# Low weight parts of layer 1 prepared during layer 0, three more root sums as split pairs, and a planner with trials

## The chip, the cores and the metric

The kernel runs on one core of one Trainium2 chip. The metric is the device time of one execution in microseconds (us). The kernel before was run three times; a profile of one further execution shows what every engine did. Engines are named as the profile names them: PE (TensorE matmul), PEld (its weight loads), DVE (VectorE), ACT (ScalarE), POOL (GpSimd) and SP (SyncE, which issues nearly all DMAs).

## The reference

A decoder trunk of two layers on 1024 tokens of width 1024, all in float32. Cut to what matters:

```python
for l in range(DEPTH):                       # 2 layers
    h = rmsnorm(x, attn_norm[l])
    proj = h @ w_in[l]                       # one input projection, split among four mixers
    y_a = mla_attention(c_q, c_kv, k_r, ...) # a: latent attention with rotary keys
    y_b = short_gated_conv(g_b, g_c, u_conv, conv_w[l])   # b
    y_c = multiscale_pool(u_pool, ...)                    # c
    y_d = swa_sink_attention(q_sw, k_sw, v_sw, ...)       # d: window of 128, with sinks
    groups = stack([y_a, y_b, y_c, y_d])     # each group of 256 channels gets its own RMS norm
    mixed = rms(groups) * mix_norm[l]
    x = x + mixed @ w_o[l]
    h2 = rmsnorm(x, ffn_norm[l])
    gate, up = split(h2 @ w_gate_up[l])
    x = x + (silu(gate) * up) @ w_down[l]
return rmsnorm(x, final_norm)
```

Every RMS norm needs, for each token, the sum of squares over the channels.

## The kernel before

**Layout and precision.** Channels lie on the 128 partitions, tokens along the free axis in two halves of 512. PE multiplies float32 matrices as split pairs: a value f becomes `hi`, its cast to the format fp32r (on ACT), and `lo = f - hi`, also in fp32r (on DVE). `mm3` (L316 to L329) makes a product of three matmuls, hi·hi, hi·lo and lo·hi. Nearly all matmuls of the kernel are issued at L322.

**Weights.** `weights` (L204 to L218) loads a block from DRAM into a place of type F, casts it to `hi` (L216, ACT) and subtracts (L217, DVE) to get `lo`. The blocks of a layer come as a stream in a fixed order (`expect_layer`, L238 to L246): 15 blocks of `w_in` (128 x 1024, 512 KB each; in layer 0 three of them are handled apart at the start), a small one for the rotary key, and 8 blocks of `w_o` (128 x 768, 384 KB). `take` and `ahead` keep one block fetched ahead; `ring_next` keeps the last two split blocks. An input block feeds both token halves, 2 x 8 x 3 = 48 matmuls.

**Places.** 47 places of 128 x 1024 float32 in SBUF hold nearly everything (class `Slots`). Each request takes a place; whoever gets a place waits for its former user.

**Root sums.** `SumSq` (L360 to L418) collects the squares in one tile per token half. `rnorm` then sums over the partitions with a matmul by a matrix of ones and computes the inverse root on ACT and DVE. Without `pair` that matmul is in fp32 (L405); with `pair`, the collected tile is split by a cast and a subtraction, and the sum is two fp32r matmuls (L402). Before the change, pairs are used for group b, the key/value latent, group a, the FFN norm and the norms after the down projection; groups c and d (`group_scale`, L738) and the query latent (`sq_q`, L868) use fp32 in both layers, and so does the first norm of the program.

**Stages of a layer.** The mixers: projections, window attention, convolution and pooling, latent attention, with the output projection in parts between them (`out_part`). Then gate-up, and then the down projection: 28 units (7 terms, B11, B21, N1, N2, T3, T4, B22, of a two-by-two block scheme that saves an eighth of the products, times 4 pairs of output blocks), each of 11 x 3 = 33 matmuls. At unit n the loop (L1784 on) issues the loads of the raw down weights of unit n + 2 (`dn_raw`, L1562), splits those of unit n + 1, fetches the next term's activations (`dn_acts`, L1597), and adds the product to the residual (L1771). In layer 0 the finished residual goes to DRAM (`done`, L1754), and the first three projections of layer 1 start within the last term.

**Order of the work.** Within the program text the order is only a draft. `scheduled_kernel` traces the program, and the class `Order` simulates it with a cost for each instruction (`costs`), a delay for DMA loads, and a model of the DMA's throughput. It lists each engine's instructions by latest start (`run`, `find`), assigns PSUM banks and places from the simulated ends, traces again, four rounds in all, and keeps the round with the shortest simulated span. The order found is imposed on every engine, SP's queue among them. All of this is done before the kernel is compiled.

Of the kernel before, what the change touches and what calls it, by code (L numbers as in the profile page):

```python
# [13 lines left out]
F32 = mybir.dt.float32  # L14
# [5 lines left out]
P = 128  # L20
# [3 lines left out]
HT = 512  # L24
# [11 lines left out]
HALVES = (1, 0)  # L36
OUT_PARTS = tuple((d, t) for d in range(NK) for t in HALVES)
N_U = 47

NSP = 3  # L40
NG = NFF // 2
# [81 lines left out]
def trunk_kernel(ctx: ExitStack, tc: tile.TileContext, ins, out, given=None, ends=None):  # L123
    nc = tc.nc
# [10 lines left out]
    R, F = View(slots, F32R), View(slots, F32)  # L135
# [65 lines left out]
        for i in ring.popleft():  # L201
            R.free_pair(i)

    def weights(src, n):  # L204
        if n > 2 * P:
            s = F.pair()
            raw = F.ap2(s)
            sp.dma_start(raw[:, :n], src)
            hi, lo = (R.ap2(i) for i in ring_next())
            F.free_pair(s)  # L210
        else:
            raw = wpool.tile([P, 2 * P], F32, name="vraw", tag="vraw")
            sp.dma_start(raw[:, :n], src)
            hi = wpool.tile([P, 2 * P], F32R, name="vhi", tag="vhi")
            lo = wpool.tile([P, 2 * P], F32R, name="vlo", tag="vlo")
        act.copy(hi[:, :n], raw[:, :n])  # L216
        dve.tensor_tensor(out=lo[:, :n], in0=raw[:, :n], in1=rd(hi[:, :n]), op=ALU.subtract)  # L217
        return hi, lo  # L218
# [16 lines left out]
    def expect(f, *args):  # L235
        stream.append((f, args))

    def expect_layer(l):  # L238
        for m in (2, 3, 0, 4, 5, 6, 1, 13, 14, 10, 11, 12, None, 7, 8, 9):
            if m is None:  # L240
                expect(rope_weights, l)
            else:
                if l or m not in (2, 3, 0):
                    expect(weights, ins["w_in"][l, m], 2 * HT)
        for d in range(NK):
            expect(weights, ins["w_o"][l, d, :, 2 * P :], 6 * P)  # L246

    def ahead():
        if stream and not fetched:
# [230 lines left out]
    for l in range(L):  # L480
# [256 lines left out]

        def group_scale(g):  # L738

            sg = SumSq(2 * P, g in "b")  # L740
            for t in range(2):
                for c in range(2):
                    sg.add(t, F.ap(y[g][c][t]))
                r = sg.rnorm(t)
                for c in range(2):
                    a = F.ap(y[g][c][t])
                    mul_to(a, a, F.ap(r))
                F.free(r)
# [116 lines left out]
                rope.append(F.half())  # L865
                sp.dma_start(F.ap(rope[-1]), ins[name][:, t * HT : (t + 1) * HT])
        cq = [[None, None], [None, None]]
        sq_q = SumSq(2 * P)  # L868
        for m in range(2):
            pp = project() if m else nextp  # L870
            for t in range(2):
# [909 lines left out]
        fresh = {B11: (0, 0), N1: (1, 1), N2: (0, 1), T4: (1, 0)}  # L1781
        banks = {}
        tail = []
        for n, (c, m) in enumerate(units):  # L1784
            if n + 2 < len(units):
                raws.append(dn_raw(*units[n + 2]))
            if c in fresh:
                u, t = fresh[c]
                d = 2 * m + u
                if not last or t == 0:  # L1790
                    x[d][t] = F.half()
                elif c == N1:
# [24 lines left out]
            evac(c, m, p)  # L1817
            for _ in range(2):
                if cn is not None and m < NM - 1:
                    nxt.extend(dn_acts(cn, (len(nxt) + 1) // 2))  # L1820
            if m == NM - 1:
                cur, nxt = nxt, []
            if c == T3:
                done(2 * m, 0)
            elif c == T4:
                done(2 * m + 1, 0)
                done(2 * m + 1, 1)
            elif c == B22:
                done(2 * m, 1)
                if m == 0:  # L1830
                    expect_layer(l + 1)
                    ahead()
                if m == 1:
                    ratt[0] = ss.rnorm(0, tag="pv")
                if m == NM - 1:
                    ratt[1] = ss.rnorm(1, tag="pv")
# [17 lines left out]
class Order:  # L1854
# [7 lines left out]
    SHARED = 1.3  # L1862
    LEAST = 0.14

    def __init__(self, traced, edges, banks=True):
        self.n = len(traced)
        self.engine = [self.queue(i) for i in traced]
        self.cost = [self.costs(i) for i in traced]
        self.kind = [self.kinds(i) for i in traced]
        self.moved = [self.passing(i) for i in traced]  # L1870
        place = {i.name: k for k, i in enumerate(traced)}
        need = [{} for _ in traced]
        users = self.users = defaultdict(list)
        for k, i in enumerate(traced):
            for m in {a.memref for a in (*i.outs, *i.ins) if hasattr(a, "memref")}:
                users[m].append(k)
        freed = [set() for _ in traced]
        for k, i in enumerate(traced):
            for name, kind in edges(i.name):
                if name in place:  # L1880
                    p = place[name]
                    need[k][p] = need[k].get(p, False) or "NoSync" not in str(kind)
                elif banks or self.engine[k] != "PE":
                    freed[k].update(place[x] for x, _ in edges(name) if x in place)
            for p in freed[k]:
                need[k][p] = True
        for m, ks in users.items():
            made = [freed[k] for k in ks if any(m == getattr(a, "memref", 0) for a in traced[k].outs)]
            for p in set().union(*made).difference(ks):
                for k in ks:  # L1890
                    if p < ks[0]:
                        need[k][p] = True
        self.need = [list(d.items()) for d in need]
        self.feeds = [[] for _ in traced]
        for k, d in enumerate(self.need):
            for p, sync in d:
                self.feeds[p].append((k, sync))
# [79 lines left out]
            return 0.29 + n * 0.00098, 0.21 + n * 0.00098  # L1977
        return t, t - 0.083

    def run(self, rank, back=False):  # L1980

        ahead, wait = (self.need, self.feeds) if back else (self.feeds, self.need)
        late, cost, kind = self.LATE[back], self.cost, self.kind
        left = [len(w) for w in wait]
        ready, end, free = [0.0] * self.n, [0.0] * self.n, dict.fromkeys(self.ENGINES, 0.0)
        later = {e: [] for e in self.ENGINES}
# [14 lines left out]
        for _ in range(self.n):  # L2004
            best = None
            for e in self.ENGINES:
                due(e, free[e])
                if not now[e] and not later[e]:
                    continue
                t = free[e] if now[e] else later[e][0][0]  # L2010
                if e == "SP" and not back and len(flying) == self.LANES:
                    t = max(t, flying[0])
                if best is None or t < best[0]:
                    best = t, e
            t, e = best
            due(e, t)
            k = heapq.heappop(now[e])[1]
            seen, taken = cost[k]
            order[e].append(k)
            if back:  # L2020
                free[e] = t + taken * (self.SHARED if kind[k] == "pool" else 1.0)
# [15 lines left out]
            for j, sync in ahead[k]:  # L2037
# [6 lines left out]
                    r = end[k] + self.HOP[e] if sync else t  # L2044
                ready[j] = max(ready[j], r)
                left[j] -= 1
                if not left[j]:
                    heapq.heappush(later[self.engine[j]], (ready[j], j))
        return end, order

    def find(self, passes=3):
        rank, best = list(range(self.n)), None
        for _ in range(passes):
# [2 lines left out]
                best = max(end), order, end  # L2056
            rank, _ = self.run([-x for x in end], back=True)
        return best

    def tiles(self, prefix):  # L2060

# [33 lines left out]
                )  # L2095


def scheduled_kernel(fresh, ins_of, rounds=4):

# [14 lines left out]
        return nc, traced, asked  # L2114

    nc, traced, asked = trace(None, None)
    plan = Order(traced, nc.dependency_edges)
    end, best = plan.find()[2], None
    for _ in range(rounds):
        given = plan.banks(end), plan.ends(end, asked)  # L2120
        nc, traced, asked = trace(*given)
        plan = Order(traced, nc.dependency_edges)
        span, order, end = plan.find()
        if best is None or span < best[0]:
            best = span, given, order
    return trace(*best[1], best[2])[0]


# [131 lines left out]
```

## Time and profile before

| | us |
|---|---|
| median of 3 runs | 2050.09 |
| lowest and highest | 2048.81, 2051.84 |
| profiled execution, its own time | 2051.07 |
| its span, first to last instruction | 2049.3 |

The profile has a page of totals and several views of the trace. A line of the view by stretches gives the stretch, its length, the busy time of each engine with its count of instructions, the granted PE clock, the DMA share (mean busy share of 16 DMA engines) and the GB/s moved. A line of the waits says who waited for whom, the sum in us, how often, and the longest. A group line has the line of the kernel, engine, operation, names of output and inputs, shapes and count, then the busy time in us and the mean duration in ns, then idle time before it and what ended that. Matmuls are pipelined: one of 512 columns is recorded with some 390 ns while the next one starts earlier, so starts are compared rather than durations.

### The profile page before, as it was taken

How to read it: one execution, taken by the hardware profiler on the slowest of the kernel's cores; microseconds unless marked ns; L12 is line 12 of the kernel's file. 1: busy time of each engine (PE TensorE's matmuls, PEld its weight loads, DVE VectorE, ACT ScalarE, POOL GpSimd, SP SyncE). 2: the span in 40 equal slices, each digit the busy share in tenths (PEclk: the TensorE clock that was granted, in tenths of full speed). 3: DMA queues.
4: the chain of work that ended last, by engine and by line, in shares of the span. 5: the costliest groups of instructions: out<-in, count | busy, mean ns of one | idle time of the engine just before them, and what ended most of it. 6: DMA issues, size and time to landing. Idle time of an engine off the chain costs nothing.

```text
span 2049.3 us, 26536 instructions
## 1 busy us (share of the span) xinstructions
PE 2029.5 (99%) x9422; PEld 1675.6 (82%) x9422; DVE 1521.4 (74%) x2443; ACT 988.8 (48%) x1737; POOL 568.7 (28%) x428
## 2 busy tenths in 40 slices
PE   9999999999999999999999999999999999999998
PEld 7887888878888888888888878888788888888887
DVE  8779978997666768655657898889966666685555
ACT  7447657753333335434433666667433333354342
POOL 0100000047786772000001000000577777710000
PEclk9999999999999999999999999999999999999999
DMA  5431232334555556766424213232455555487552
GB/s 203 97 76 41 74 104 79 141 134 154 199 174 187 180 167 250 269 217 197 157 59 94 52 52 102 74 108 110 150 176 187 176 175 176 162 298 258 178 188 87
DMA packets 144294, 305.51 MB, mean 149 GB/s; under 512 B 13985, under 2 KB 61089, under 8 KB 144161
## 3 DMA queue, kind: packets, MB, share of 16 engines
q1 hardware_dynamic: 139680, 292.27, 41.8%
q0 software_dynamic: 4480, 11.54, 3.2%
q8 instruction: 74, 1.21, 0.2%
q14 instruction: 60, 0.48, 0.1%
HBM read 219.34 MB, written 94.90 MB: 153 GB/s over the span
## 4 chain that ended last, share of the span: by engine, by line
PE 91%; DVE 5%; issue 1%; DMA 1%; ACT 1%; POOL 0%; SPq 0%; DVEq 0%; ACTq 0%; POOLq 0%
PE ps_mm L322 35%; PE ps_s L322 28%; PE ps_t L322 10%; PE ps_pv L322 8%; PE ps_pv L1090 2%; PE ps_t L1078 1%; DVE u L345 1%; PE ps_s L1024 1%; PE ps_s L1026 1%; PE ps_s L1025 1%; DMA u<-in_w_gu 1%; PE ps_s L896 1%; DVE u L348 1%; PE ps_pv L699 1%; PE ps_s L638 1%
## 5 line engine op out<-in xcount | busy, mean ns | idle before, releaser
L322 PE MATMUL ps_mm<-u,u 128*128 128x512 f32 (+1 forms) x3378 | 833.3, 390 | 4.4 <-ACT u L342 1.5
L322 PEld LDWEIGHTS ps_mm<-u,u 128*128 128x128 f32 x3378 | 615.0, 188 | 131.3 <-issue 5.5
L322 PE MATMUL ps_s<-u,u 128*128 128x512 f32 x2670 | 634.4, 390 | 2.8 <-DVE u L345 1.7
L345 DVE TENSOR_TENSOR u<-u,u 128x1024 fp32r<-128x1024 f32 (+2 forms) x400 | 453.3, 1152 | 231.6 <-ACT u L342 161.1
L322 PEld LDWEIGHTS ps_s<-u,u 128*128 128x128 f32 x2670 | 500.4, 188 | 110.8 <-DVE u L345 4.0
L342 ACT CAST u<-u 128x1024 fp32r<-128x1024 f32 (+2 forms) x400 | 345.8, 882 | 456.2 <-PE ps_mm L322 72.1
L322 PE MATMUL ps_t<-u,u 128*128 128x512 f32 (+1 forms) x1124 | 254.2, 378 | 1.1 <-DVE u L1309 1.1
L322 PEld LDWEIGHTS ps_t<-u,u 128*128 128x128 f32 x1124 | 202.1, 188 | 41.7 <-DVE u L1309 1.6
L1502 POOL TENSOR_TENSOR tp<-tp,u 128x512 f32<-128x512 f32 x80 | 126.3, 1579 | 345.0 <-ACT tp L1500 345.0
L322 PE MATMUL ps_pv<-u,u 128*128 128x512 f32 x744 | 177.1, 389 | 0.0
L322 PEld LDWEIGHTS ps_pv<-u,u 128*128 128x128 f32 x744 | 139.6, 188 | 29.1
L296 POOL DMA_DIRECT2D gd<-in_w_gu x24 | 22.1, 921 | 421.5 <-PE ps_t L322 283.9
L1087 POOL MEMSET u<- 128x128 f32 x32 | 6.1, 221 | 431.3 <-PE ps_pv L1090 148.8
L1500 ACT ACTIVATE tp<-tp 128x512 f32<-128x512 f32 x80 | 50.6, 632 | 147.9 <-DVE tp L421 147.8
L347 ACT ACTIVATE u<-u,par 128x512 fp32r<-128x512 f32 x100 | 70.4, 717 | 37.4 <-DVE u L421 11.0
L342 ACT CAST u<-ps_t 128x512 fp32r<-128x512 f32 (+3 forms) x132 | 65.1, 503 | 47.9 <-PE ps_t L1078 26.7
L348 DVE SCALAR_TENSOR_TENSOR u<-u,par,u 128x512 fp32r<-128x512 f32 x100 | 73.3, 745 | 17.6 <-ACT u L347 17.4
L345 DVE TENSOR_TENSOR u<-ps_t,u 128x512 fp32r<-128x512 f32 (+3 forms) x132 | 75.4, 580 | 12.7 <-ACT u L342 10.9
L1580 POOL TENSOR_TENSOR u<-u,u 128x352 f32<-128x352 f32 x64 | 82.7, 1293 | 2.9 <-DMA u<-in_w_dn 1.5
L1580 POOL TENSOR_TENSOR u<-u 128x352 f32<-128x352 f32 x64 | 82.1, 1284 | 4.6 <-DMA u<-in_w_dn 3.9
L386 ACT ACTIVATE tn<-u 128x512 f32<-128x512 f32 (+1 forms) x91 | 52.9, 596 | 57.2 <-DVE u L1771 47.9
L1290 POOL TENSOR_TENSOR u<-u 128x512 f32<-128x512 f32 x38 | 69.5, 1829 | 21.8 <-DVE u L345 21.8
(203 smaller groups left out, 2347.4 us busy)
## 6 DMA issues: line engine op xcount, KB each, us to landing
u<-in_w_gu SPq DMA_DIRECT2D x84, 512.0 KB, 4.2
ad<-u SPq DMA_DIRECT2D x154, 256.0 KB, 2.4
u<-ad SPq DMA_DIRECT2D x70, 512.0 KB, 4.7
u<-in_w_dn SPq DMA_DIRECT2D x64, 352.0 KB, 3.6
qd<-u SPq DMA_DIRECT2D x64, 352.0 KB, 2.6
u<-qd SPq DMA_DIRECT2D x32, 512.0 KB, 5.0
u<-in_w_in SPq DMA_DIRECT2D x28, 512.0 KB, 3.5
u<-in_w_dn SPq DMA_DIRECT2D x24, 512.0 KB, 5.2
```

Of the source, the lines that this page charges most:

```text
L296: paced(pool.dma_start(d, a, **more))
L322: last_mm = pe.matmul(o, w, r, start=start and k == 0 and i == 0, stop=stop and k == n - 1 and i == 2, skip_group_check=again,)
L342: a = act.copy(hi, f)
L345: dve.tensor_tensor(out=lo, in0=f, in1=rd(hi), op=ALU.subtract)
L347: a = act.activation(hi, f, AF.Copy, scale=gain)
L348: dve.scalar_tensor_tensor(out=lo, in0=f, scalar=gain, in1=rd(hi), op0=ALU.mult, op1=ALU.subtract)
L386: act.activation(q, f, AF.Square)
L1090: pe.matmul(py[:, c0:], v_of(j, h), R.ap(s)[:, c0:], start=j == 0 and n == 0, stop=j == nj - 1 and n == 1,)
L1290: pool.tensor_tensor(out=q4, in0=q4, in1=F.ap(self.raw[1] + 1), op=ALU.add)
L1500: last_silu = act.activation(g, g, AF.Silu)
L1502: pool.tensor_tensor(out=g, in0=g, in1=r, op=ALU.mult)
L1580: pool.tensor_tensor(out=o, in0=a, in1=b, op=ALU.add)
```

## The change

It has three parts.

1. `prepare` loads a weight block of layer 1, splits it, and stores its `lo` to a DRAM tile of its own; the `hi` is dropped. The down stage of layer 0 calls it 23 times, for 15 blocks of `w_in` and 8 of `w_o`, about once per unit from unit 2 to unit 26. In layer 1, `weights` then loads the raw block and the stored `lo` by two DMAs, casts `hi` and leaves out the subtraction. Layer 0's own weights are split as before.
2. In layer 1, the root sums of groups c and d and of the query latent are made as split pairs. Each has two token halves.
3. The planner makes one round for each of two assumed speeds (DVE and ACT as modelled, and 3% slower). Each order is then changed at random 30 times, by shifting the ranks of instructions that end shortly before a wait of PE (`improve`), a change being kept if the simulated span is no longer. Of the two, the one with the shorter mean span in six simulations of the fixed order is taken, in which a quarter of the DMA loads are late by up to 2.5 us and the engines' costs vary by 2% (`trial`).

```diff
+SLOW = (1.0, 1.03)
+PREP = (1, 27)
...
+    prepared = {}
+
+    def prepare(key, src, n):
+
+        s, h, lo = F.pair(), R.pair(), R.pair()
+        raw = F.ap2(s)[:, :n]
+        sp.dma_start(raw, src)
+        split(R.ap2(h)[:, :n], R.ap2(lo)[:, :n], raw)
+        F.free_pair(s)
+        R.free_pair(h)
+        prepared[key] = dpool.tile([P, n], F32, name="ph%s%d_%d" % key)
+        sp.dma_start(prepared[key], rd(R.ap2(lo)[:, :n]))
+        R.free_pair(lo)
+
-    def weights(src, n):
+    def weights(src, n, key=None):
         if n > 2 * P:
             s = F.pair()
             raw = F.ap2(s)
             sp.dma_start(raw[:, :n], src)
             hi, lo = (R.ap2(i) for i in ring_next())
             F.free_pair(s)
+            if key in prepared:
+                sp.dma_start(rd(lo[:, :n]), prepared[key])
+                act.copy(hi[:, :n], raw[:, :n])
+                return hi, lo
...
-            sg = SumSq(2 * P, g in "b")
+            sg = SumSq(2 * P, g in ("b", "bcd")[l])
...
-        sq_q = SumSq(2 * P)
+        sq_q = SumSq(2 * P, l > 0)
...
+        todo = deque() if last else deque([*(("in", m) for m in (2, 3, 0, 4, 5, 6, 1, 13, 14, 10, 11, 12, 7, 8, 9)), *(("o", d) for d in range(8))])
         for n, (c, m) in enumerate(units):
+            while not last and n > PREP[0] and len(todo) * (PREP[1] - PREP[0]) > 23 * (PREP[1] - n) and todo:
+                w, i = todo.popleft()
+                src = ins["w_in"][l + 1, i] if w == "in" else ins["w_o"][l + 1, i, :, 2 * P :]
+                prepare((w, l + 1, i), src, 2 * HT if w == "in" else 6 * P)
...
+    def trial(self, order):
+        ends = (self.run(None, fixed=order, draw=random.Random(n))[0] for n in range(6))
+        return sum(map(max, ends)) / 6
...
+    def improve(self, best, tries):
+        draw = random.Random(1)
+        span, order, end = best
+        rank, _ = self.run([-x for x in end], back=True)
+        e, o = self.run(rank)
+        if max(e) <= span:
+            span, order, end = max(e), o, e
+        found = self.waits(order, end)
+        for _ in range(tries):
+            at = draw.choices([t for t, _ in found], [w for _, w in found])[0]
+            new = [
+                r + draw.gauss(0.0, 1) if at - 40 < t < at + 5 else r for r, t in zip(rank, end)
+            ]
+            e, o = self.run(new)
+            if max(e) <= span:
+                rank, span, order, end = new, max(e), o, e
+                found = self.waits(order, end)
+        return span, order, end
...
-def scheduled_kernel(fresh, ins_of, rounds=4):
+def scheduled_kernel(fresh, ins_of, rounds=1):
...
+    for slow in SLOW:
+        plan, asked, first.slow = first, tried, slow
+        end = plan.find()[2]
+        for _ in range(rounds):
+            given = plan.banks(end), plan.ends(end, asked)
+            nc, traced, asked = trace(*given)
+            plan = Order(traced, nc.dependency_edges, slow)
+            best = plan.find()
+            end = best[2]
+            order = plan.improve(best, 30)[1]
+            found.append((plan.trial(order), given, order))
+    best = min(found, key=lambda x: x[0])
     return trace(*best[1], best[2])[0]
```

More of the change, by code (lines that the diff above doesn't have):

```diff
@@ L2 @@
 import math
+import random
 from collections import defaultdict, deque
@@ L243, in expect_layer @@
                 if l or m not in (2, 3, 0):
-                    expect(weights, ins["w_in"][l, m], 2 * HT)
+                    expect(weights, ins["w_in"][l, m], 2 * HT, ("in", l, m))
         for d in range(NK):
-            expect(weights, ins["w_o"][l, d, :, 2 * P :], 6 * P)
+            expect(weights, ins["w_o"][l, d, :, 2 * P :], 6 * P, ("o", l, d))
     def ahead():
@@ L1863, with __init__ @@
     LEAST = 0.14
-    def __init__(self, traced, edges, banks=True):
+    def __init__(self, traced, edges, slow=1.0, banks=True):
+        self.slow = slow
         self.n = len(traced)
@@ L1978, in costs, with run @@
         return t, t - 0.083
-    def run(self, rank, back=False):
+    def run(self, rank, back=False, fixed=None, draw=None):
         ahead, wait = (self.need, self.feeds) if back else (self.feeds, self.need)
         late, cost, kind = self.LATE[back], self.cost, self.kind
+        if fixed is None:
+            cost = [
+                (a * self.slow, b * self.slow) if e in ("DVE", "Activation") else (a, b)
+                for (a, b), e in zip(cost, self.engine)
+            ]
         left = [len(w) for w in wait]
@@ L2006, in run @@
             for e in self.ENGINES:
[L2007 to L2010, printed above, removed]
+                if fixed is not None:
+                    i = len(order[e])
+                    if i == len(fixed[e]) or left[fixed[e][i]]:
+                        continue
+                    t = max(free[e], ready[fixed[e][i]])
+                else:
+                    due(e, free[e])
+                    if not now[e] and not later[e]:
+                        continue
+                    t = free[e] if now[e] else later[e][0][0]
                 if e == "SP" and not back and len(flying) == self.LANES:
@@ L2015, in run @@
             t, e = best
-            due(e, t)
-            k = heapq.heappop(now[e])[1]
-            seen, taken = cost[k]
+            if fixed is not None:
+                k = fixed[e][len(order[e])]
+            else:
+                due(e, t)
+                k = heapq.heappop(now[e])[1]
+            seen, taken = cost[k]
+            if draw:
+                late = 2.5 * draw.random() if draw.random() < 0.25 else 0.0
+                if e in ("DVE", "Activation", "Pool"):
+                    more = draw.gauss(0.0, 0.02) * seen
+                    seen, taken = seen + more, taken + more
             order[e].append(k)
@@ L2046, in run @@
                 left[j] -= 1
-                if not left[j]:
+                if not left[j] and fixed is None:
                     heapq.heappush(later[self.engine[j]], (ready[j], j))
         return end, order
+    def trial(self, order):
+        ends = (self.run(None, fixed=order, draw=random.Random(n))[0] for n in range(6))
+        return sum(map(max, ends)) / 6
     def find(self, passes=3):
@@ L2058, in find, with waits @@
         return best
+    def waits(self, order, end):
+        found, free = [], 0.0
+        for k in order["PE"]:
+            seen, taken = self.cost[k]
+            start = end[k] - seen
+            if start - free > 0.05:
+                found.append((start, start - free))
+            free = start + taken
+        return found
+    def improve(self, best, tries):
[10 more added lines that the diff above has]
+                r + draw.gauss(0.0, 1) if at - 40 < t < at + 5 else r for r, t in zip(rank, end)
+            ]
+            e, o = self.run(new)
[3 more added lines that the diff above has]
+        return span, order, end
     def tiles(self, prefix):
@@ L2116, in scheduled_kernel @@
     nc, traced, asked = trace(None, None)
[L2117 to L2125, printed above, removed]
+    first, tried, found = Order(traced, nc.dependency_edges), asked, []
+    for slow in SLOW:
[10 more added lines that the diff above has]
+    best = min(found, key=lambda x: x[0])
     return trace(*best[1], best[2])[0]
```

## Prediction

> **What bounds the kernel now.** I read the totals of the page first, then its engines by stretch, then the list of TensorE's waits, and only then single instructions.
>
> ```profile
> PE 2029.5 (99%) x9422; PEld 1675.6 (82%) x9422; DVE 1521.4 (74%) x2443; ACT 988.8 (48%) x1737; POOL 568.7 (28%) x428
> PEclk9999999999999999999999999999999999999999
> ```
>
> TensorE (PE) is busy for 2029.5 of 2049.3 us at the full granted clock. Busy time alone does not prove that it runs at its best rate, so the stretches come next: layer 0's mixers (50 to 430), its gate-up stage (450 to 800), its down stage (811 to 1021), the inner part of that, and layer 1's mixers (1021 to 1440). The columns after the length are PE, PEld, DVE, ACT, POOL, then clock, DMA share and GB/s.
>
> ```profile
> 50.00:430.00 380.00, 377.98 (x1851) 311.10 (x1849) 331.27 (x735) 235.60 (x510) 19.78 (x30) 1.00 0.30 87
> 450.00:800.00 350.00, 350.00 (x1541) 288.58 (x1540) 247.59 (x247) 122.49 (x168) 248.74 (x173) 1.00 0.53 180
> 811.00:1021.00 210.00, 210.00 (x928) 173.85 (x927) 128.27 (x154) 96.35 (x127) 1.81 (x1) 1.00 0.64 218
> 827.00:1015.00 188.00, 188.00 (x831) 155.62 (x830) 112.69 (x137) 84.13 (x113) 0.00 (x0) 1.00 0.62 207
> 1021.00:1440.00 419.00, 415.54 (x2016) 341.31 (x2014) 346.56 (x752) 247.41 (x527) 16.81 (x30) 1.00 0.28 82
> ```
>
> In gate-up 1541 matmuls of 512 columns take 350 us: 0.227 us each, with no gap. The down stage runs at the same rate, 210 / 928 = 0.226 us. PE stands still only in the mixers, 380 - 378.0 = 2.0 us in layer 0 and 419 - 415.5 = 3.5 us in layer 1, and at the two ends of the program. So time can be won in two ways only: fewer or cheaper matmuls, or fewer of these gaps. All of PE's waits are in this list (us in total, times, longest); it has 15 groups, of which these are the larger ones and the last:
>
> ```profile
> PE ps_s L322 <- DVE u L345: 1.7, 3, 1.1
> PE ps_mm L322 <- ACT u L342: 1.5, 2, 0.8
> PE ps_t L322 <- DVE u L1309: 1.1, 1, 1.1
> PE ps_pv L541 <- DVE ones L145: 1.1, 1, 1.1
> PE ps_mm L322 <- DVE te L421: 0.8, 3, 0.5
> PE ps_s L322 <- DVE u L1228: 0.7, 1, 0.7
> PE ps_s L409 <- ACT tn L408: 0.6, 1, 0.6
> ...
> PE ps_mm L322 <- DVE u L1106: 0.2, 1, 0.2
> ```
>
> The 15 groups add up to 10.6 us. The 1.1 us before the first matmul (L541) and the 0.6 us in the last sum (L409) are chains with nothing to put beside them; about 9 us of gaps are left that another order or a less loaded engine could touch. No group names a DMA, and none names line 217, the subtraction that the change takes out of layer 1.
>
> **The change, part by part.** First, the root sums, the one part that changes PE's own work. A sum over 128 partitions is one fp32 matmul with ones (L405, two records) or two fp32r matmuls with the split pair (L402). Both stand in layer 1:
>
> ```profile
> 1187.57 0.62 PE L402 MATMUL ps_t<-u,ones_r 128*128 128x512 f32 x2
> 1188.03 1.77 PE L896 MATMUL ps_s<-u,u 128*128 128x512 f32 x7
> 1203.78 1.12 PE L405 MATMUL ps_t<-u,ones 128*128 128x512 f32 x2
> 1204.34 0.79 PE L322 MATMUL ps_mm<-u,u 128*128 128x512 f32 x1
> 1204.97 0.62 PE L322 MATMUL ps_s<-u,vhi 128*128 128x512 f32 x2
> ...
> 1209.81 1.02 PE L405 MATMUL ps_t<-u,ones 128*128 128x512 f32 x2
> 1210.27 1.94 PE L322 MATMUL ps_mm<-u,u 128*128 128x512 f32 x6
> ```
>
> The pair holds PE from 1187.57 to 1188.03, 0.46 us. From the fp32 sum at 1203.78 to the second matmul behind it at 1204.97 it is 1.19 us, of which 0.23 is the one ordinary matmul: 0.96 us. For the sum at 1209.81, the six matmuls behind it end at 1212.21; with five of them at 0.227 and the last one's 0.39 us it is 2.40 - 1.14 - 0.39 = 0.87 us. The change makes three sums of layer 1 pairs (groups c and d, and the query latent), each in two halves of the tokens: six matmuls, each 0.41 to 0.50 us shorter, together 2.5 to 3.0. I take **-2.7 us**.
>
> Each of the six also adds a cast and a subtraction of 512 columns ahead of the sum, at the price of these rows (layer 1, names then count, busy, mean ns):
>
> ```profile
> L342 ACT CAST u<-u 128x512 fp32r<-128x512 f32 x13 | 8.1, 624 | 22.8 <-DVE u L844 12.5 <-DVE u L818 6.6 <-DVE u L388 2.1
> L345 DVE TENSOR_TENSOR u<-u,u 128x512 fp32r<-128x512 f32 x13 | 8.9, 684 | 0.9 <-ACT u L342 0.7
> L217 DVE TENSOR_TENSOR u<-u,u 128x1024 fp32r<-128x1024 f32 x11 | 13.4, 1218 | 0.2 <-ACT u L216 0.2
> L217 DVE TENSOR_TENSOR u<-u,u 128x768 fp32r<-128x768 f32 x8 | 7.6, 952 | 0.0
> ```
>
> That is 0.62 + 0.68 = 1.3 us more before a root is there, against 0.4 to 0.5 us less in the sum. Hidden if other matmuls stand ready, which in the rows above they do: PE goes from the sum straight to the next projection. If that cover is gone for all six, the loss is 6 x 0.85 = 5.1 us. I take 0 and keep 0 to 5.1.
>
> Second, the subtractions leave layer 1. Line 217 has 11 instructions of 1.22 us and 8 of 0.95 us in its mixers, 13.4 + 7.6 = 21.0 us of VectorE (DVE); six new subtractions give back 6 x 0.68 = 4.1. DVE goes from 346.6 to about 330 of 419 us. The weights ring needs its low part 1.2 us earlier than before only if a projection waits for it, and no group of PE's waits says so. DVE's gaps are waits for other results that come 1 us late on a busy DVE. The gain is therefore bounded by nothing and by the 3.5 us of gaps in this stage; five per cent off DVE's load makes 0.5 to 1 us of them, and I take -0.8. The low part comes by its own DMA instead: 23 loads more, at 82 GB/s and a DMA share of 0.28, behind the high part's. A load of that size lands in 3.5 us by its row below and a weight feeds 48 matmuls, 10.9 us. If the ring's place came free too late, one load would cost PE up to 3.5 us; I take 0.
>
> Third, the 23 preparations (15 input blocks of 512 KB, 8 output blocks of 384 KB) go into layer 0's down stage, about one per unit of 33 matmuls (33 x 0.227 = 7.5 us). What they issue: a load, a cast, a subtraction and a store each.
>
> ```profile
> L345 DVE TENSOR_TENSOR u<-u,u 128x1024 fp32r<-128x1024 f32 x55 | 67.1, 1231 | 42.2 <-ACT u L342 31.7 <-PE ps_s L322 6.7 <-PE ps_pv L322 2.0
> L342 ACT CAST u<-u 128x1024 fp32r<-128x1024 f32 x55 | 57.4, 1051 | 57.2 <-DMA u<-ad 23.8 <-PE ps_mm L322 8.3 <-PE ps_s L322 8.3
> u<-in_w_in SPq DMA_DIRECT2D x28, 512.0 KB, 3.5
> SPq L1754 <- DVE u L1771: 27.5, 12, 7.6
> 810.00:820.00 10.00, 10.00 (x46) 8.27 (x45) 9.14 (x11) 9.19 (x10) 1.81 (x1) 1.00 1.03 410
> 840.00:850.00 10.00, 10.00 (x46) 8.29 (x45) 8.35 (x10) 4.09 (x5) 0.00 (x0) 1.00 0.97 333
> ```
>
> DVE gets 15 x 1.23 + 8 x 0.95 = 26.1 us and stands at 128.3 + 26.1 = 154 of 210; ScalarE (ACT) at 15 x 1.05 and three quarters of that for the 8, some 22 us, goes to 119 of 210. Both stay hidden behind PE. The stores wait on the subtraction in SyncE's (SP's) queue, and behind them stand the loads of the next unit's weights (L1562) and activations (L1597). SP already waits in this way for the residual's stores, 27.5 us in 12 times and up to 7.6 us, with no gap on PE, because weights are asked for two units, 15 us, ahead. So cost 0 for the engines.
>
> The DMA is closer. 15 x 2 x 0.524 + 8 x 2 x 0.393 = 22.0 MB are added to 207 GB/s x 188 us = 38.9 MB: 60.9 MB in 188 us, **324 GB/s**. The trace has 410 GB/s over 10 us and 333 GB/s at a share of 0.97, PE at full rate in both. It just fits; taken 0, bounds below.
>
> The rule that speaks against the change: the Trainium skill, HBM Reference, section "Specifications (TRN2)", states an effective bandwidth of some 358 GB/s per core, a core's half of its domain. The 410 GB/s of the row above is over it, as that section allows for a core that streams alone. By 358 the four units of the term T4, 2.95 MB each as counted below, would take 8.2 us instead of 7.5, an estimate of 3 us for the four and a sum of -1.7 instead of -4.7.
>
> Fourth, the planner. It is run offline and adds no instruction, but every engine's order, the PSUM banks and the places change: one round instead of four, for two speeds of DVE and ACT, each bettered by 30 random trials around PE's waits, the choice by six runs with jitter. It can only move the 9 us of gaps. Two stages of one kind under one planner show what an order is worth: 2.0 us of gaps in layer 0's mixers, 3.5 in layer 1's. Bounds: all 9 us away, or 3 us more (1.5 us per mixer stage). I take -1.2, as much as bringing layer 1 near to layer 0.
>
> **The sum**: -2.7 - 0.8 - 1.2 = -4.7 us. The profiled execution took 2051.07 us (its span 2049.3 and 1.8 us around it), 1.0 us over the median 2050.09 of the three runs; 2051.07 - 4.7 = 2046.4 in its terms, and **2045.4** as a median.
>
> **The rivals.**
>
> Only the sums pay (2047.4). For it: no wait of PE names line 217, so DVE's relief may be worth nothing, and a random search may find nothing that holds on the chip. Against: DVE ends most of PE's gaps. 2050.1 - 2.7 = 2047.4.
>
> The gaps mostly go (2043). For it: they are few and short, and the search aims at them. Against: their ends are chains (L1309, L345) without other work beside. 2.7 and half of 9 make -7.2.
>
> DMA becomes the bound in the down stage (2056, slower). The mechanism: a unit needs 0.72 MB of down weights, in all but the last term 0.72 MB of the next term's activations, in N1, N2 and T3 0.26 MB of residual, in T4 0.79 MB, and now 0.7 to 0.96 MB of preparation. That is some 2.65 MB per unit in N1, N2 and T3 and 2.95 MB in T4. At 333 GB/s these take 8.0 and 8.9 us against 7.5: 12 x 0.5 + 4 x 1.4 = 11.6 us late by the end of T4. It decides once the lead of two units, 15 us, is eaten otherwise, for instance by a store at the head of SP's queue for 7.6 us together with preparations issued before urgent loads. Then some 10.5 us appear as waits of PE on DMA: 2050.1 - 4.7 + 10.5 = 2056. Against: the 410 GB/s row, and the last term B22, which loads no activations and gives the time back.
>
> The new order is worse (2050.4): -2.7 and 3 us more gaps, one round instead of four being a weaker start.
>
> That the change does less than it says: if the low parts are not taken from DRAM, line 217 keeps its 19 instructions in layer 1 and only the first rival's sum is left.
>
> **How the numbers follow.** A measurement of this kernel can tell about 0.2%, 4.1 us, from no change: the line lies at 2046.0. Forecast 0.40, its own spread 2043.9 to 2047, of which 0.28 is below the line; only the sums 0.22; gaps mostly gone 0.17; DMA the bound 0.12; order worse 0.09, a third of it over 2054.2. Faster: 0.28 + 0.17 = 0.45. Same: 0.12 + 0.22 + 0.06 = 0.40. Slower: 0.12 + 0.03 = 0.15. The range goes from 2041.5, the far side of the gaps, to 2051.5, which covers the worse order's middle and leaves out the DMA case and a little on both sides, under 0.2.
>
> **What would show each step.** Sums: L402 on ps_t with 12 records more, L405 on ps_t with 12 fewer (28 to 16), and next to each pair 0.46 us on PE. Subtractions: line 217's place in layer 1 empty at 1024 and 768 columns, DVE near 330 us there. Preparations: 23 stores and loads of new DRAM tiles, the down stage's DVE near 154 us, its GB/s near 320, and PE still at 0.226 us per matmul; a group "PE <- DMA" or a down stage over 210 us means the DMA rival. Planner: the sum of PE's waits, below 10.6 us if right. I would be wrong above all if the transfers delay weights, or if the new order opens gaps where the trace has none now.

## The result, and the profile after

The changed kernel takes 2038.91 us (median of 6, 2038.71 to 2039.19) against 2049.69 for the kernel before (6 runs): a ratio of 0.9947, interval 0.9934 to 0.9959. That is 10.8 us less where 4.7 were forecast, and below the range. The profiled execution took 2038.94 us with a span of 2037.2, 12.1 us under the span before.

PE's total on the page after, and three stretches of it that hold the same work as those shown of before (layer 0's mixers, its down stage, layer 1's mixers; columns as there). Lines of the changed kernel lie 21 further down: L343 is the former L322, L366 the former L345, L423 and L426 the former L402 and L405, L238 the former L217.

```profile
PE 2023.3 (99%) x9422; PEld 1677.9 (82%) x9422; DVE 1543.7 (76%) x2449; ACT 1015.1 (50%) x1766; POOL 564.1 (28%) x428
```

```profile
50.00:428.00 378.00, 376.68 (x1848) 311.01 (x1846) 329.92 (x734) 235.63 (x511) 18.14 (x29) 1.00 0.30 87
809.00:1019.00 210.00, 210.00 (x928) 173.85 (x927) 147.24 (x174) 116.58 (x149) 1.81 (x1) 1.00 0.92 331
1019.00:1428.00 409.00, 408.07 (x2006) 339.99 (x2005) 328.19 (x739) 249.67 (x532) 15.13 (x29) 1.00 0.35 106
```

The count of matmuls is the same, 9422. The down stage still runs 928 matmuls in 210 us although its DMA went from 218 to 331 GB/s: in that stage the preparations are free. DVE there is at 147 us where 154 were forecast, and in layer 1's mixers at 328 us, as forecast (330). What got shorter is the mixers, layer 1's above all.

All of PE's waits after:

```profile
PE ps_pv L562 <- DVE ones L148: 1.1, 1, 1.1
PE ps_mm L343 <- ACT u L368: 0.7, 2, 0.6
PE ps_mm L343 <- DVE tn L435: 0.6, 1, 0.6
PE ps_s L430 <- ACT tn L429: 0.6, 1, 0.6
PE ps_s L343 <- ACT u L1339: 0.5, 2, 0.3
PE ps_mm L343 <- ACT u L363: 0.4, 1, 0.4
PE ps_mm L343 <- DVE u L369: 0.3, 1, 0.3
PE ps_s L343 <- DVE u L366: 0.2, 1, 0.2
PE ps_s L1045 <- DVE te L442: 0.2, 1, 0.2
```

They add up to 4.6 us instead of 10.6. With 2.5 us for the sums (the instructions and counts below) that makes 8.5 of the 12.1 us of span. The rest is time in which PE counts as busy. These two rows cut the same 2012 matmuls of layer 1 (one more or less at the edge) out of the trace of before and of the trace after:

```profile
1029.50:1450.10 420.60, 415.56 (x2012) 340.39 (x2011) 348.67 (x757) 247.68 (x529) 20.34 (x32) 1.00 0.28 83
```

```profile
1026.90:1437.80 410.90, 409.70 (x2011) 341.06 (x2010) 332.90 (x746) 249.95 (x536) 18.62 (x31) 1.00 0.35 105
```

The stretch is 9.7 us shorter. PE's idle time fell from 5.0 to 1.2 us, 3.8. Its busy time fell by 5.9, and the sums explain 2.5 of that; 3.4 us were delays recorded as busy. A matmul of 512 columns is recorded with 390 ns and the next one is due 227 ns after its start, so a start up to 163 ns late leaves no idle time, and every longer wait is listed 163 ns too short. (The Trainium skill, Perfetto Trace Analysis, section "Identifying the Most-Contended Engine", holds matmul busy time to be a poor measure of how near a kernel is to its limit, because matmuls are pipelined; this trace agrees, with these 3.4 us.) Taken over the whole trace (each matmul's start to the next one's, less the time at full rate for its shape: 227 ns for 512 columns, 120 for 256, 109 for 128, 870 for an fp32 sum), what PE lost went from 39.8 to 30.2 us: 1.3 less in the first 200 matmuls, 1.1 less in layer 0's mixers, 7.2 less in layer 1's, and the rest unchanged, some 10 us at the program's end included. (Half a nanosecond more or less for each of the 8166 matmuls of 512 columns moves both totals by 4 us; their difference stays.)

The sums and the new DMAs in the trace after, by line (engine, operation, tiles and count: shortest, median and longest ns) and by issue (count, size, us to landing in the down stage):

```profile
L426 PE MATMUL ps_t<-u,ones x16: 590/592/697, 20.4 to 196.6; 128*128 128x512 f32 x16
...
L423 PE MATMUL ps_t<-u,ones_r x40: 389/392/476, 172.4 to 1409.5; 128*128 128x512 f32 x40
```

```profile
phin<-u SPq DMA_DIRECT2D x15, 512.0 KB, 5.6
...
pho<-u SPq DMA_DIRECT2D x8, 384.0 KB, 4.9
```

The fp32 records on ps_t went from 28 to 16 and those of pairs from 28 to 40, as foretold: six sums at 0.41 us less. No fp32 sum is left behind 196.6 us except at the program's end.

### The profile page after: what moved, and what is told of

Read it like the earlier page. It is cut to its first block, busy times and chain, and to the rows that moved or that the text cites. A ratio compares the mean times of both kernels' runs of the same rounds, so it can differ in the third digit from the quotient of the medians.

```text
span 2037.2 us, 26750 instructions
## 1 busy us (share of the span) xinstructions
PE 2023.3 (99%) x9422; PEld 1677.9 (82%) x9422; DVE 1543.7 (76%) x2449; ACT 1015.1 (50%) x1766; POOL 564.1 (28%) x428
## 4 chain that ended last, share of the span: by engine, by line
PE 97%; DVE 1%; issue 1%; ACT 0%; DMA 0%; POOL 0%; SPq 0%; DVEq 0%; ACTq 0%; POOLq 0%
PE ps_mm L343 38%; PE ps_s L343 29%; PE ps_t L343 12%; PE ps_pv L343 8%; PE ps_pv L1111 2%; PE ps_t L1099 1%; PE ps_s L1045 1%; PE ps_s L1047 1%; PE ps_s L1046 1%; PE ps_s L659 1%; PE ps_s L917 1%; PE ps_pv L720 1%; PE ps_t L708 1%; PE ps_t L423 0%; DVE u L366 0%
## 5 line engine op out<-in xcount | busy, mean ns | idle before, releaser
L343 PE MATMUL ps_mm<-u,u 128*128 128x512 f32 (+1 forms) x3378 | 831.9, 389 | 2.1 <-ACT u L368 0.7
L343 PEld LDWEIGHTS ps_mm<-u,u 128*128 128x128 f32 x3378 | 616.1, 188 | 125.4 <-issue 2.4
L343 PE MATMUL ps_s<-u,u 128*128 128x512 f32 x2670 | 636.4, 390 | 0.7 <-ACT u L1339 0.5
L366 DVE TENSOR_TENSOR u<-u,u 128x1024 fp32r<-128x1024 f32 (+3 forms) x429 | 493.8, 1174 | 187.4 <-ACT u L363 131.1
L363 ACT CAST u<-u 128x1024 fp32r<-128x1024 f32 (+3 forms) x429 | 370.6, 883 | 443.4 <-PE ps_mm L343 62.8
L343 PEld LDWEIGHTS ps_s<-u,u 128*128 128x128 f32 x2670 | 500.9, 188 | 107.0 <-ACT u L1339 1.3
L343 PE MATMUL ps_t<-u,u 128*128 128x512 f32 (+1 forms) x1124 | 256.3, 378 | 0.1
L343 PEld LDWEIGHTS ps_t<-u,u 128*128 128x128 f32 x1124 | 202.5, 188 | 40.8 <-DVE u L1515 1.5
L343 PE MATMUL ps_pv<-u,u 128*128 128x512 f32 x744 | 177.1, 389 | 0.0
L343 PEld LDWEIGHTS ps_pv<-u,u 128*128 128x128 f32 x744 | 139.7, 188 | 29.0
L366 DVE TENSOR_TENSOR u<-ps_t,u 128x512 fp32r<-128x512 f32 (+3 forms) x132 | 74.7, 580 | 13.3 <-ACT u L363 12.4
L1601 POOL TENSOR_TENSOR u<-u 128x352 f32<-128x352 f32 x64 | 77.0, 1204 | 8.6 <-DMA u<-in_w_dn 8.1
L1601 POOL TENSOR_TENSOR u<-u,u 128x352 f32<-128x352 f32 x64 | 76.4, 1194 | 2.7
L442 DVE TENSOR_TENSOR tp<-tp,u 128x512 f32<-128x512 f32 x76 | 75.3, 990 | 2.0
```

The lines of the kernel that those rows point to most:

```text
L343: last_mm = pe.matmul(o, w, r, start=start and k == 0 and i == 0, stop=stop and k == n - 1 and i == 2, skip_group_check=again,)
L363: a = act.copy(hi, f)
L366: dve.tensor_tensor(out=lo, in0=f, in1=rd(hi), op=ALU.subtract)
L442: dve.tensor_tensor(out=o, in0=a, in1=b, op=ALU.mult)
L1601: pool.tensor_tensor(out=o, in0=a, in1=b, op=ALU.add)
```

## Experiments: which part did it

The first four took the three parts apart. Each was timed against the kernel before on the same chip (2050.21 us there).

**plan_only**: the changed kernel's planner on the work of before.

```diff
-        todo = deque() if last else deque([...])
+        todo = deque()
-            sg = SumSq(2 * P, g in ("b", "bcd")[l])
+            sg = SumSq(2 * P, g in "b")
-        sq_q = SumSq(2 * P, l > 0)
+        sq_q = SumSq(2 * P)
```

> The new planner alone: no preparation, root sums as before. The changed kernel is 10.8 us under the one before, of which the six root sums explain 2.5; some 8 us came from PE's delays. Theory A (the planner's order took the delays away): 2042 to 2044, 6 to 8 us under the kernel before. Theory B (a less loaded DVE in layer 1 took them away): 2048 to 2050, at most 2 us under. Both: about 2046.

Measured: 2040.1 us (2039.57 to 2040.79), ratio 0.9952 (0.9938 to 0.9966). Theory A, and 2 us more than it asked: the planner alone is worth 10 us.

**prep_sums_old_plan**: the preparation and the sums, with the class `Order` and `scheduled_kernel` of before.

```diff
-def scheduled_kernel(fresh, ins_of, rounds=1):
+def scheduled_kernel(fresh, ins_of, rounds=4):
-    for slow in SLOW:
...
+    for _ in range(rounds):
```

> Preparation and root sums with the planner of before (four rounds, no trials). Theory A (planner): only the sums pay, 2047 +- 1. Theory B (DVE relief): 2040 to 2042. My own recorded terms, sums 2.7 and relief 0.8, would make 2046.

Measured: 2047.84 us (2046.51 to 2048.81), ratio 0.9987 (0.9978 to 0.9996). No more than the sums' 2.5 us; of DVE's relief nothing can be told.

**plan_prep** leaves out the sums alone, **plan_sums** the preparation alone.

```diff
 plan_prep:
+            sg = SumSq(2 * P, g in "b")
+        sq_q = SumSq(2 * P)
 plan_sums:
+        todo = deque()
```

> Planner and preparation, root sums as before (fp32). If the sums are worth their 2.5 us on PE and nothing else: 2041.4, 2.5 over the changed kernel. If the 1.3 us longer chain ahead of a split sum costs something, the difference is smaller than 2.5; if shorter sums also remove waits behind them, larger.

> Planner and root sums, no preparation. Theory A (planner): within 2 us of the changed kernel, 2039 to 2041. Theory B (DVE relief): 2045 to 2048, since layer 1's DVE then carries 21 us more.

Measured: plan_prep 2041.51 us (2040.7 to 2042.87), 2.6 over the changed kernel: the sums are worth their 2.5 us there. But plan_sums takes 2045.04 us (2043.55 to 2047.58), 5 us more than plan_only, with less work on PE. That is the lower edge of theory B's range, but plan_only, which gives DVE as little relief, rules theory B out as it stood. The largest wait of PE in its trace, then SP's waits around it, then the stretch behind the wait:

```profile
PE ps_mm L343 <- ACT u L237: 2.9, 1, 2.9
```

```profile
SPq L225 <- DVE u L366: 32.3, 2, 24.2
...
SPq L225 <- PE ps_t L423: 2.6, 2, 2.2
```

```profile
1189.70:1193.10 3.40, 3.40 (x9) 2.61 (x9) 3.37 (x6) 1.75 (x4) 0.00 (x0) 0.51 0.52 136
```

A weight block's load (L225) stands at the head of SP's queue for 24.2 us behind a split's subtraction on DVE and then 2.2 us behind the matmuls of a root sum's pair (L423), until these give its place free; PE then waits 2.9 us for the block's cast (L237). Behind the wait the granted clock falls to 0.51 for 3.4 us, in which PE makes 9 matmuls where 15 fit at 0.227 us. Counted from start to start, this one spot (1180 to 1200 us) costs 5.7 us, where the same 20 us of plan_only cost 0.2; elsewhere in layer 1's mixers plan_sums loses about as much as plan_only (5.6 and 5.1 us). Without its 5.5 us plan_sums would stand at some 2039.5, an estimate, and no longer above plan_only. DVE is no fuller ahead of it than in the changed kernel: 26.2 of the 27 us from 1155 to 1182, beside 26.1. To see whether the late load is one order's accident, **plan_sums_seed2** takes another seed for the trials, and **all_seed2** does so for the changed kernel.

```diff
-        draw = random.Random(1)
+        draw = random.Random(2)
```

> Planner and sums without preparation, another seed. In the first order one weight block came late and PE waited 2.9 us for its cast. If that was this order's accident: 2037.5 to 2041. If DVE's load in layer 1 without preparation makes such waits: 2044 or more again.

> The changed kernel with another seed for the 30 trials, so the same work in another order. It tells how far an order found by chance moves the time. If orders of one planner are alike: 2038 to 2040. If they scatter as planner with sums alone against the others suggests (5 us over what its work would give): anywhere from 2037 to 2044.

Measured: 2046.11 us (2044.68 to 2047.45) and 2039.46 us (2038.71 to 2040.01). The changed kernel's time does not hang on its seed, and plan_sums_seed2 has the same wait of 2.9 us. But the seed hardly changes an order: in the traces DVE's instructions follow each other alike in both runs of plan_sums, but for one of 2449, and in both of the changed kernel, but for 35. So this is one order twice, and an accident of that order is not ruled out. Shown is that the sums pay in the changed kernel and that one late load took more than they are worth in plan_sums; that it was late for want of the preparation is not shown.

## Experiments: what in the planner

**plan_improve** keeps the 30 random trials and drops the second speed (and with it the choice); **plan_choice** drops the trials and keeps both speeds. Both do the work of before, and the kernel before took 2049.48 us beside them.

```diff
 plan_improve:
-SLOW = (1.0, 1.03)
+SLOW = (1.0,)
 plan_choice:
-            order = plan.improve(best, 30)[1]
+            order = plan.improve(best, 0)[1]
```

> The work of before, a planner of one round at the modelled speed and 30 random trials around PE's waits; no second speed and so no choice. If the trials are what took PE's delays away: 2039.5 to 2041.5, as the whole planner alone (2040.1). If the slower assumed speed or the choice by jitter did it: 2046 or more.

> The work of before, one round at each of the two speeds, no random trials, the choice by the six runs with jitter. If the trials do it: 2047 to 2051. If the choice or the second speed does it: 2040 to 2042.

Measured: 2049.91 us, ratio 1.0002 (0.9993 to 1.001), and 2040.8 us, ratio 0.9956 (0.9944 to 0.9969). The random trials bring nothing, at 3% no more than here (plan_only 2040.1 with them, plan_choice 2040.8 without); all of it comes from the order planned at 3% slower, which is the one that the choice takes: in the traces DVE's sequence in plan_choice agrees with plan_only's in 2264 of 2443 instructions, and with that of plan_improve, which is planned as modelled, in only 1587. The same stretch of layer 1 as above, first of plan_improve, then of plan_choice, with the same work in both:

```profile
1028.20:1448.90 420.70, 415.52 (x2012) 340.32 (x2011) 348.71 (x757) 247.21 (x528) 19.95 (x32) 1.00 0.29 83
```

```profile
1026.60:1439.30 412.70, 412.02 (x2011) 341.31 (x2010) 345.70 (x757) 246.45 (x529) 18.24 (x31) 1.00 0.30 85
```

8.0 us less for the same 2012 matmuls, at nearly the same DVE and ACT time: 4.5 of them were idle time and 3.5 delay inside busy time. plan_improve's list of waits still has the groups of before: ps_s for DVE's L366 with 1.7 us, ps_s for L1249 and ps_t for L1330 with 1.0 each, ps_mm for L442 with 0.8. plan_choice's list has only the first of these four, at 0.6 us.

Is 3% a margin, or was it a lucky draw? **speed_097**, **speed_1015** and **speed_106** plan the work of before at one speed, without trials.

```diff
-SLOW = (1.0, 1.03)
+SLOW = (0.97,)          # 1.015 and 1.06 in the other two
```

> The work of before, one round, no trials, planned as if DVE and ACT were 3% faster than modelled. Theory M (an order planned with a margin for DVE and ACT survives the chip, one planned without does not): 2049 to 2054, no better than before. Theory C (every order is another draw and 1.03 drew well): as likely 2040 as 2050.

> The same, planned with DVE and ACT 1.5% slower. Theory M: between, 2043 to 2048. Theory C: no order among the speeds.

> The same, planned with DVE and ACT 6% slower. Theory M: 2038 to 2042, as at 3% (2040.8 with the choice, which took the 3% order). Theory C: anywhere from 2038 to 2050.

| assumed DVE and ACT time | 0.97 | 1.0 (plan_improve) | 1.015 | 1.03 (plan_choice) | 1.06 |
|---|---|---|---|---|---|
| us | 2060.37 | 2049.91 | 2045.21 | 2040.80 | 2043.45 |

The times fall in order up to 3% and rise a little at 6%. That is what theory M asks, and a lottery would hardly do it. Two sizes were missed: 0.97 is 6.4 us over its band and 6% is 1.5 us over. By stage the curve is that of layer 1's mixers, where PE loses, from start to start and in the order of the table, 14.6, 13.5, 9.0, 5.6 and 5.8 us; in layer 0's it loses 16.6, 8.6, 9.5, 7.4 and 9.3, with no order from 1.0 on. Each speed is a single order, so where between 1.5 and 6% the best lies is not told.

Through what does the margin act? **places_103** uses 1.03 only in the simulation that assigns places and PSUM banks, **order_103** only in the one that orders the engines; **dve_103** and **act_103** use it in both, but for one engine.

```diff
 places_103:
-            plan = Order(traced, nc.dependency_edges, slow)
+            plan = Order(traced, nc.dependency_edges)
 order_103:
-        plan, asked, first.slow = first, tried, slow
+        plan, asked = first, tried
 dve_103 (act_103 with "Activation"):
-                (a * self.slow, b * self.slow) if e in ("DVE", "Activation") else (a, b)
+                (a * self.slow, b * self.slow) if e == "DVE" else (a, b)
```

> The work of before, one round, no trials. Places and banks from a simulation at 1.03, the imposed order from one at 1.0. If the margin acts through the order: 2047 to 2052. If through places and banks: 2040 to 2043.

> The opposite: places and banks from a simulation at 1.0, the imposed order from one at 1.03. If the margin acts through the order: 2040 to 2043. If through places and banks: 2047 to 2052.

> Both at 1.03 for DVE alone, ACT as modelled. DVE is the fuller engine in the mixers (347 of 419 us against ACT's 247), so if its margin is what counts: 2040 to 2043. If ACT's casts, which come ahead of DVE's subtractions, need the margin: 2046 or more.

> The work of before, one round, no trials, places and order from a simulation with ACT 3% slower and DVE as modelled. If the two margins add: 2045 to 2047 (DVE alone 2044.3, both 2040.8, none 2050). If ACT's margin only helps beside DVE's: 2049 or more.

Measured, against 2049.63 for the first three and 2050.16 for the last: places 2046.75 (ratio 0.9983, 0.9974 to 0.9993), order 2048.08 (0.9992, 0.9983 to 1.0001), DVE 2044.28 (0.9976, 0.9965 to 0.9986), ACT 2045.11 (0.9974, 0.9965 to 0.9984). Either half of the planning alone gives 1.5 us (not told from none) to 3 us, both together 9: my either-or was wrong, the gain comes where the order and the places are planned at the same speed. DVE's run fell between its two bands. The two engines' margins about add in total, 5.4 and 5.1, but not by stage: in layer 1's mixers PE loses 6.1 us with DVE's margin alone and 8.8 with ACT's (13.5 with none, 5.6 with both), and in layer 0's 11.2 and 10.3 (8.6 and 7.4). In layer 1 DVE's margin alone brings nearly all, so that the totals add is in part chance.

## Experiments: the rival in the DMA, and better versions

**prep_squeezed** presses the 23 preparations into twelve units; **layer0_sums** makes the same three sums of layer 0 pairs; **all_104** plans the changed kernel at 4%.

```diff
 prep_squeezed:
-PREP = (1, 27)
+PREP = (1, 14)
 layer0_sums:
+            sg = SumSq(2 * P, g in "bcd")
+        sq_q = SumSq(2 * P, True)
 all_104:
-SLOW = (1.0, 1.03)
+SLOW = (1.04,)
```

> The changed kernel with its 23 preparations pressed into units 2 to 13 instead of 2 to 26. 22 MB more in some 90 us beside 207 GB/s ask for about 450 GB/s, over the 410 GB/s that the trace of before has for 10 us. If the DMA can become the bound and delays reach PE: 2045 to 2055, waits of PE on DMA in the down stage. If the two units of lead and the planner's order absorb it: 2038 to 2040, as the changed kernel.

> The changed kernel with layer 0's sums of groups c and d and of the query latent as split pairs too: six fp32 sums fewer, 2.5 us of PE, and six casts and subtractions more in layer 0's mixers (DVE 330 of 378 us there). If the order keeps the new chains off PE's path: 2036.5. If a fuller DVE in layer 0 costs as much: 2039 or more, as in the run with sums and no preparation.

> The changed kernel planned at 4% only, 30 trials. If the best margin lies between 3 and 6%: 2036 to 2038.5, better than both kernels. If 3% is about the best: 2039 to 2041.

prep_squeezed: 2038.67 us (2038.5 to 2038.93), as the changed kernel. In its trace the DMA engines are full for 100 us, and PE loses nothing:

```profile
825.00:925.00 100.00, 100.00 (x443) 82.85 (x442) 74.38 (x83) 61.21 (x74) 0.00 (x0) 1.00 1.03 411
```

443 matmuls in 100 us is 0.226 us each. The rival's mechanism does not set in even at twice the density: the DMA is at its limit, and still no weight came too late for PE.

layer0_sums: 2043.27 us (2043.11 to 2043.6), 4.4 over the changed kernel, although PE has 2.5 us less to do. Layer 0's mixers in its trace, and the same matmuls after:

```profile
47.90:431.70 383.80, 379.85 (x1863) 312.52 (x1861) 336.03 (x745) 241.08 (x522) 18.77 (x30) 1.00 0.31 87
```

```profile
48.30:429.70 381.40, 379.66 (x1863) 313.14 (x1860) 333.25 (x739) 238.38 (x516) 18.98 (x30) 1.00 0.30 88
```

Idle time rose from 1.7 to 4.0 us and what the sums saved in busy time is gone too: 2.4 us longer where 2.5 less were due. Layer 0's weights are not prepared, and its DVE is fuller. With plan_sums that makes two orders, one in each layer, in which the sums cost time where no subtractions had been taken from DVE. That a fuller DVE is the cause is not shown. Between 140 and 200 us PE waits for weights being split (0.4 us for L238, 0.2 for L237; the changed kernel has no wait there) and loses 2.5 us more than the changed kernel from start to start. But as much more is lost between 220 and 260 us (4.4 against 1.9), and there all_104, with layer 0's sums in fp32, loses 4.5 too, up to 1.7 of it at half the clock (see below): an order can lose as much there without the sums.

all_104: 2038.34 us (2037.76 to 2038.89), ratio 0.994 (0.9926 to 0.9953), beside 0.9947 (0.9934 to 0.9959) for the changed kernel: within the band for a best margin between 3 and 6%, but no difference that these intervals can tell. In its profiled execution the granted clock fell to 0.50 for 3.4 us behind a wait of 1.2 us in layer 0, up to 1.7 us that this order need not lose. No version tried beats the changed kernel clearly.

## Why the prediction was wrong

**What bounds the kernel** was read rightly: PE, at full rate wherever it was fed, with the mixers' delays as the only other thing to win.

**The sums** (-2.7) were right: 2.5 on PE by their shapes and counts, 2.6 in time between plan_prep and the changed kernel. That their longer chain costs nothing held in the changed kernel. plan_sums, without the preparation, took 5 us more than plan_only, and that this is the size of the upper bound that was kept (5.1) is chance: its loss is not the chain ahead of six roots but one weight block that got its place late. Such a load had been priced at up to 3.5 us, for the low parts of the changed kernel, and taken as 0.

**The relief of DVE** (-0.8) was not found as a term of its own: plan_prep is 1.4 us over plan_only, and with the old planner preparation and sums together brought 2.4. Beside the sums the preparation makes some 6 us (2045.0 and 2046.1 without, 2038.9 with), but that is the one late load of one order, and the runs do not show that DVE's load made it late. The parts do not simply add, because each change of the work also changes the order.

**The preparations** (0) were right, and the DMA rival, the only one on the slower side, has no place: 331 GB/s here and 411 in the squeezed run, with no wait of PE in that stage. (Its 10.5 us also do not follow from the 11.6 worked out for it.) Its 333 GB/s had been read from a stretch that was not at its limit. The 358 GB/s per core of the Trainium skill (HBM Reference, "Specifications (TRN2)"), which would have cost 3 us, are passed too, by the 411 of that row, as the section's sentence on a core that streams alone allows.

**The planner** (-1.2) is the step that failed. "It can only move the 9 us of gaps" took the list of waits for the whole of PE's delay. By starts PE lost 39.8 us, and the changed kernel lost 9.6 less, of which 3.6 never stood in a list. And the size was taken from how two stages differ under one planner, which says nothing of what a planner with a margin does. I looked to the random trials for the gain; they are worth nothing (plan_improve), and the 3% is worth nearly 9 (plan_choice). Of the rivals, "the gaps mostly go" was nearest in kind and still 4 us short.

What stays open is why a simulation at the modelled speed makes an order that does not hold. Some modelled costs are too low: a scaled subtraction of 512 columns (L348) is modelled at 0.15 + 512 x 0.00109 = 0.708 us and the page of before has 745 ns. But a plain one is modelled at 0.685 us and has 684. That the margin covers such misses and the DMA's scatter is an argument; the runs show only that it works, by how much, and for both engines. A part of the gain may need no margin: simulated with the costs as modelled and nothing late, the planner's own order made at 3% ends after 2024.6 us and the one made at 1.0 after 2026.7 (worked out from the kernel texts of the speed runs, off the chip). By the model too it is the better order, by 2 of the 9 us; the other 7 the model does not see.

## What to carry to other kernels

Where one engine is full and an offline planner orders the rest, plan the others a few per cent slower than they are, in every simulation that the plan is made of, and measure the curve; here 3% on DVE and ACT was worth more than everything done to the work. Count a full engine's losses from start to start at the known rate, since a list of waits leaves out what pipelining hides. And where parts do not add, look first at where the time is lost: here one late load made up the whole difference between two versions.

## What the runs showed of the hardware

The DMA engines moved 411 GB/s for 100 us at a share of 1.03 while PE ran at 0.226 us per matmul, so the 410 GB/s in one stretch of before were no short peak; no 10 us from 800 to 940 in prep_squeezed stand above 416. A share of 0.97 at 333 GB/s had looked like the limit and was not. A load of 512 KB of activations took 4.7 us to land over the whole program before and 5.8 after. Behind a wait of PE of 2.9 us (plan_sums, at 1189 us) and one of 1.2 us (all_104, at 241 us) the granted clock stood at half for 3.4 us, so these two waits cost up to 1.7 us more than their length; behind order_103's waits of up to 1.3 us it did not fall.
